# A fused hybrid decoder layer: the order of every engine listed operation by operation, and the places of its rotating buffers listed too

## The chip, the cores and the metric

One core of one Trainium2 chip runs the whole kernel. The metric is the device time in microseconds; the median of three runs of the kernel before is 687.27 us (686.93 to 688.39). The core has five engines that run side by side, each through its own list of instructions: TensorE (PE, matrix products and transposes by a product with the identity), VectorE (DVE), ScalarE (ACT), GpSimd (POOL) and SyncE (SP, which here issues most transfers). An engine takes its instructions strictly in the order of its list and waits on semaphores for what the others produce.

## The reference

One decoder layer for 1024 positions of width 1024, all in float32. A modulation is computed from a conditioning vector, the input is normalised and modulated, and one projection gives the queries, three sets of keys and values, gates, and the input of a state-space mixer. Two mixers follow: attention with three branches (compressed, selected and window keys), 8 heads of 64 in two groups, and a diagonal complex recurrence with 32 groups of 64 states. Both are gated, put side by side, projected, and added to the input.

```python
mod = jax.nn.silu(c) @ w_ada + b_ada
shift, scale, gate = jnp.split(mod, 3, axis=-1)
h = rms_norm(x, norm_g) * (1 + scale[:, None, :]) + shift[:, None, :]
proj = h @ w_in
...
q = rms_norm(q.reshape(B, T, N_HEADS, HEAD_DIM), q_norm_g)
kc = rms_norm(compress(kv_heads(kcr), cmp_pos_k, cmp_w1_k, cmp_w2_k), k_cmp_norm_g)
...
attn = nsa_attention(q, kc, vc, k_slc, kv_heads(vsl), k_win, kv_heads(vwn), gates)
attn = attn * jax.nn.silu(z_a)
y = s5_mixer(u, ssm_a_re, ssm_a_im, ssm_log_dt, ssm_b_re, ssm_b_im, ssm_c_re, ssm_c_im, ssm_d)
y = jax.nn.gelu(y)
y = y * jax.nn.sigmoid(y @ glu_w.astype(jnp.float32) + glu_b.astype(jnp.float32))
ssm = y.astype(x.dtype) * jax.nn.silu(z_s)
mix = jnp.concatenate([attn, ssm], axis=-1) @ w_out
return x + gate[:, None, :] * mix
```

With 16 selected blocks of 64 positions, all 1024 positions are selected, so the selected branch is plain causal attention.

## The kernel before

Most large products are made in three pieces: each float32 operand is split into a rounded part and the rest (names ending in `hi`/`h` and `lo`/`l`), and the products high by high, high by low and low by high are summed in PSUM. So one 128x512 result of eight contraction steps takes 24 matmuls.

The work is cut into 680 jobs, registered by name with the jobs they need (`I("kpan0", ...)`). The names that matter here, in the order of the program:

- Start: `sc0`, `sc1` make silu of the conditioning vector on every partition (`sc`); `ma`, `mb`, `mc` load and use the modulation weights `wada` (a 128x1024 product with `sc`, summed along the row by DVE; `gs` and `sh` are the scale and shift that come of it); `sq0` to `sq7` square rows of x for the norm (some on DVE, some on ACT), `xsc0` and `xsc1` scale x by the norm (L156 on DVE, L258 on ACT), `xb` transposes it on PE (`ptr`, L266) and `h00` to `h71` evacuate it as `hhi`, `hf` (L297) and `hlo`.
- Projections: `kvaw0..7` and `qaw0..7` split weights (`wsp`, L209 on ACT for the high part), `kva`, `kvb`, `qa`, `qb` are the key/value and query products (`ptp`, L331 to L333), `u0` to `u3`, `cmpk`, `cmpv` and `z` use another layout (`pcp`, L352). `kpan0` norms the first keys and rotates them (`ropeb` on DVE, `kr` on POOL, L152); `kpat0` transposes them on PE (`pkt`, L480).
- State-space mixer, for four groups s: `prep`, `tab`, `mats` prepare its matrices (`s5W`, `s5T`, `s5CA`), `scan` runs the recurrence on DVE (`z`), `out` multiplies with it on PE: `py` takes one product with `s5T` (L853) and one with `z` and `s5CA` (L854) for each of eight groups.
- Attention, per row block i and head h: `ha` are the score products (`S`, L1171) and the row maxima on DVE (`st`, L1188), then the exponentials on ACT (`pp`, L1204); `hs` the sums' reciprocals, `hb` and `hc` normalise both branches into `hl` (L1223 on ACT, L149 on DVE) and issue DMA transposes of it (`PT`, from SP); `ub` the products of V with `PT` (`po`, L1264), many small ones by head; `qt` transposes queries, `ca` and `ct` are the compressed branch (`pc`, `mc`, `Sc`, `lc`). Row blocks go 0, 1, 2, 3, 7, 6, 5, 4.
- Output: `wo` splits and gates the output weights (L152 on DVE), `so`, `at` and `ao` are the output products of the two halves (`po`, L1054).

What sets the order: the list `ORD` names the jobs, and their code runs in that order. The tile framework's scheduler then orders each engine's instructions by its own costs, under the data dependencies. Only the start is pinned: `in_order(sp)` holds SP's order from the first load to job `sw`, and `in_order(dve, act)` DVE's and ACT's to job `eo`. Rotating buffers (19 of tag `w4`, 13 of `w2`, 6 of `f2`, two score banks `S` in PSUM, and others) are taken in turn by tag; a tile waits until the tile before it in its place has been read.

Of the kernel before, what the change touches and what calls it, by code (L numbers as in the profile page):

```python
# [21 lines left out]
NT = 8  # L22
# [10 lines left out]
cU3 mats1 xl1 kpat1 kvb7 kpb0 tq kpb1 kpbn0 u2 qaw0 u3 mod0 mod1 prep2 kpbn1 tab1 cVC out0 scan1 out1 tab2 xl2 cmpk
qaw1 cmpv kpbt0 qaw2 mod2 mod3 mod4 mats2 hidk qaw3 qaw4 qaw5 qa0 qa1 qa2 kpbt1 qa3 mod5 qa4 qa5 qaw6 mod6 qaw7 qa6
qa7 qp0 qp1 qpn0 qs0 qpn1 prep3 qs1 tab3 hidv xl3 qw0 scan2 qr0 cz0 mats3 qw1 scan3 qb0 gw qb1 gates mod7 modf cok cov
cmpK z0_0 qb2 scalev qb3 z0_1 qb4 z0_2 out2 qb5 qb6 g2 cz2 qr1 cz1 z0_3 qt01 qt00 qb7 qpb0 qpb1 qpbn0 ca0 qpbn1 z0_4
z0_5 z0_6 z0_7 out3 cz3 kt ha00 ha01 hs01 ha02 hb00 hc00 z1_0 z1_1 ha03 hs03 hb01 hb02 z1_2 z1_3 z1_4 qsb1 qsb0 z1_5
# [12 lines left out]
hb62 ub75 ha64 hc61 hc62 hb63 ha65 ub76 hs65 so4 hb64 hb65 ha66 ha67 ub77 ca5 ub60 ub61 hc63 hc64 so5 qt50 ub62 ha50  # L50
qt51 hs67 hb66 hb67 hc65 qw4 qr4 ub63 so7 hc66 ha51 hc67 hs51 ub64 hb50 hb51 hc50 hc51 so6 ha52 ha53 ha54 ha55 ha56
ub65 hs53 hb52 hb53 ub66 so3 wo00 wo01 wo02 wo03 ct5 hc52 qt41 at3 hc53 ub67 ub50 hs55 hb54 hb55 hc54 ha57 hs57 ca4
ao30 hc55 ao31 ao00 ao01 qt40 hb56 hb57 at1 at2 ao10 ha40 ha41 hs41 hb40 hc56 hb41 hc57 hc40 ha42 ub51 ao11 ha43 ub52
ao20 hs43 hb42 ct4 hb43 hc41 hc42 ao21 ha44 ha45 hc43 ub53 hs45 ub54 at7 ao70 hb44 hb45 ub55 ao71 ha46 ub56 ub57 ub40
at5 at6 ha47 ao50 ao51 ao61 hc44 hs47 ub41 hc45 hb46 hc46 hb47 ao60 ub42 ub43 ub44 ub45 ub46 hc47 ub47 lo
# [11 lines left out]
    wo13="d", xa0="d", xa1="d", xa2="t", xa3="d", xa4="d", xa5="d", xa6="d", xa7="d")  # L67
N4, N2, F2 = 19, 13, 6
# [11 lines left out]

@with_exitstack
def hymba(ctx: ExitStack, tc: tile.TileContext, t, out, dbg=None):
    nc = tc.nc
    pe, act, dve, pool, sp = nc.tensor, nc.scalar, nc.vector, nc.gpsimd, nc.sync
# [36 lines left out]
    def pst(n, name, tag):  # L121
        return psum["pool"].tile([128, n], F32, name=name, tag=tag, bufs=psum[tag])
# [64 lines left out]
    start = ctx.enter_context(ExitStack())  # L187
    start.enter_context(in_order(sp))
# [276 lines left out]
    def kv_norm(kk, i, r1):  # L465
# [7 lines left out]
        rope(kr, k8, lambda k: cs[:, k, i:i + 2, None, :])  # L473
# [417 lines left out]
    def cmp_hidden(b, nm):  # L891
# [14 lines left out]
        pb_ = ws([128, 2], F32, "pb_")  # L906
# [84 lines left out]
    def y_prep(hf, s):  # L991

        if (s, hf) == (0, 0):
            M["y"] = {}
        if hf == 0:
            M["y"][s] = s4([128, 2, 512], F32, "y", 0)
        u_ = f2([128, 512], F32, "pu_")
        y_ = f2([128, 512], F32, "py_")
        dma(y_[:], yd[s][:, 4 * hf:4 * hf + 4, :].rearrange("p i j -> p (i j)"), "e")
        act.activation(u_[:], y_[:], AF.Square, scale=math.sqrt(0.044715))  # L1000
        stt(u_[:], u_[:], 1.0, y_[:], OP.add, OP.mult)
        act.activation(u_[:], u_[:], AF.Tanh, scale=math.sqrt(2.0 / math.pi))
        stt(M["y"][s][:, hf], u_[:], 1.0, y_[:], OP.add, OP.mult)
# [23 lines left out]
    def gate_row():  # L1027
        M["gate"] = gate = cur["f2"].tile([128, 1024], F32, name="gate")
# [337 lines left out]
    first_ = ExitStack()  # L1366
    first_.enter_context(in_order(dve, act))
# [31 lines left out]
    I("eo")(lambda: first_.close())  # L1399
# [114 lines left out]
    def second_pool():  # L1514
        nonlocal pb
# [12 lines left out]
    I("sp", "sw", "u7m", "gates", "qa7", "qb7", "kva7", "kvb7", "u2", "u3", "cmpk", "cmpv", *zall)(second_pool)  # L1528
# [35 lines left out]
    did = set()  # L1564
# [5 lines left out]
    assert did == set(it), set(it) - did  # L1570
# [58 lines left out]
```

## Time and profile before

| what | value |
| --- | --- |
| median of three runs | 687.27 us (686.93 to 688.39) |
| profiled execution, span from its first to its last instruction | 685.9 us |
| mean granted TensorE clock over the span | 0.984 of full speed |
| instructions | 12622 |
| POOL, busy | 152.5 us |
| HBM read, written | 58.10 MB, 18.61 MB |

The trace gives one execution, and no other time of it than the span; around the span lie some 1.4 us of the median. A row of waits reads: engine, what it was about to make and the line, what it waited for, then us in all, times, longest. A row of a timeline reads: start, duration, engine, line, operation, result and operands, and in brackets the idle time before it and what ended it. A matmul's duration overlaps the next one's, so spacing of starts is the measure of its rate.

### The profile page before, as it was taken

The page shows a single profiled execution, that of the slowest core. Times are in us where ns is not written, and L with a number is a line of the kernel's source. Part 1 is how long each engine was busy: PE and PEld are TensorE (multiplying, and loading weights), DVE is VectorE, ACT ScalarE, POOL GpSimd, SP SyncE. Part 2 cuts the span into 40 slices and gives each one's busy share as a digit, 9 for nine tenths or more (in the row PEclk, how much of TensorE's full clock was granted, in tenths as well). Part 3 has the DMA queues.
Part 4 walks back from the last instruction along what each step waited for, and adds up shares of the span by engine and source line. Part 5 has one row for each costly group of instructions (what it writes and reads, how often), then busy time and mean ns, then how long its engine had stood idle before and what let it go on. Part 6 is the DMA issues. An engine that isn't in the chain of part 4 may idle for free.

```text
span 685.9 us, 12622 instructions
## 1 busy us (share of the span) xinstructions
PE 622.1 (91%) x4662; PEld 492.2 (72%) x4662; DVE 570.0 (83%) x1107; ACT 377.1 (55%) x732; POOL 152.5 (22%) x162
## 2 busy tenths in 40 slices
PE   2578998999798999899999999998899999799996
PEld 0356786887687887788788787657687877687785
DVE  6998999688936889986677787998999998898873
ACT  2777432643472152546577586676766855756641
POOL 0163309129232020460111101112001220011010
PEclk9989999999999999999999999999999999999999
DMA  8984222336275642383556969569979599698994
GB/s 319 417 254 101 47 66 55 98 114 172 68 246 169 181 128 70 89 258 93 133 136 111 223 157 205 155 171 221 235 171 215 127 231 225 166 225 197 252 223 86
DMA packets 209759, 116.76 MB, mean 170 GB/s; under 512 B 159073, under 2 KB 188513, under 8 KB 209698
## 3 DMA queue, kind: packets, MB, share of 16 engines
q1 hardware_dynamic: 205858, 109.38, 62.8%
q0 software_dynamic: 3840, 6.57, 4.2%
q8 instruction: 37, 0.61, 0.4%
q14 instruction: 24, 0.20, 0.1%
HBM read 58.10 MB, written 18.61 MB: 112 GB/s over the span
## 4 chain that ended last, share of the span: by engine, by line
PE 45%; DVE 32%; DMA 8%; ACT 6%; issue 6%; POOL 1%; SPq 1%; DVEq 0%; ACTq 0%; POOLq 0%
PE pcp L352 14%; PE po L1054 8%; PE S L1171 7%; DVE hl L149 5%; DMA wada<-in_w_adaT_dram 3%; PE po L1264 3%; DVE st L1188 3%; PE pglu L1016 3%; DVE z L152 2%; DVE wada L149 1%; PE ptp L333 1%; DVE ps L152 1%; PE ptp L332 1%; ACT pp L1204 1%; PE ptp L331 1%
## 5 line engine op out<-in xcount | busy, mean ns | idle before, releaser
L1204 ACT ACTIVATE pp<-S,st 128x640 f32<-128x640 f32 (+7 forms) x128 | 88.6, 700 | 52.1 <-DVE st L1188 40.8
L149 DVE SCALAR_TENSOR_TENSOR hl<-pp,st,hl 128x640 f16<-128x640 f32 (+7 forms) x128 | 101.2, 822 | 6.2 <-ACT hl L1223 6.1
L1223 ACT ACTIVATE hl<-pp,st 128x640 f16<-128x640 f32 (+7 forms) x128 | 85.3, 731 | 8.3 <-DVE st L152 6.3
L1054 PE MATMUL po<-wo,oh 128*128 128x512 f32 x264 | 85.3, 408 | 4.6 <-DVE wo L152 2.9
L352 PE MATMUL pcp<-hhi,wh 128*128 128x512 f32 x208 | 85.1, 409 | 1.3 <-ACT G L887 1.0
L352 PE MATMUL pcp<-hlo,wh 128*128 128x512 f32 x208 | 82.8, 398 | 0.0
L352 PE MATMUL pcp<-hhi,wl 128*128 128x512 f32 x208 | 82.7, 397 | 0.0
L1188 DVE TENSOR_REDUCE st<-S 128x1 f32<-128x1024 f32 (+3 forms) x64 | 57.1, 917 | 3.8 <-PE S L1171 3.7
L1171 PE MATMUL S<-kT,qh 128*128 128x128 f32 (+3 forms) x192 | 59.4, 368 | 0.8 <-ACT pp L1204 0.7
L1054 PEld LDWEIGHTS po<-wo,oh 128*128 128x128 f32 x264 | 48.8, 191 | 15.7 <-DVE wo L152 4.0
L1264 PE MATMUL po<-V,PT 128*128 128x64 f16 x1584 | 59.2, 193 | 0.5 <-DMA PT<-hl 0.5
L331 PE MATMUL ptp<-wsp,hhi 128*128 128x512 f32 x128 | 54.0, 424 | 5.2 <-ACT hhi L297 3.1
L1264 PEld LDWEIGHTS <-PT 128*128 128x128 f16 x1584 | 53.9, 98 | 6.5 <-issue 5.1
L333 PE MATMUL ptp<-wsp,hlo 128*128 128x512 f32 x128 | 54.1, 424 | 3.1 <-POOL hlo L152 3.1
L332 PE MATMUL ptp<-wsp,hhi 128*128 128x512 f32 x128 | 53.8, 420 | 1.9 <-DVE wsp L152 1.0
L1171 PE MATMUL S<-kT,ql 128*128 128x128 f32 (+3 forms) x192 | 53.8, 339 | 0.1
L152 POOL TENSOR_TENSOR qr<-ropeb 128x512 f32<-128x512 f32 x16 | 23.2, 1467 | 125.2 <-DVE ropeb L152 61.6
L1054 PE MATMUL po<-wo,ol 128*128 128x512 f32 x120 | 47.9, 401 | 0.0
L352 PEld LDWEIGHTS pcp<-hhi,wh 128*128 128x128 f32 x208 | 39.6, 190 | 10.1 <-ACT G L887 1.4
L352 PEld LDWEIGHTS pcp<-hlo,wh 128*128 128x128 f32 x208 | 39.2, 189 | 9.2
L352 PEld LDWEIGHTS pcp<-hhi,wl 128*128 128x128 f32 x208 | 39.4, 189 | 8.2
L1171 PEld LDWEIGHTS S<-kT,qh 128*128 128x128 f32 x192 | 33.2, 190 | 14.6 <-issue 9.8
(328 smaller groups left out, 1361.1 us busy)
## 6 DMA issues: line engine op xcount, KB each, us to landing
wada<-in_w_adaT_dram SPq DMA_DIRECT2D x24, 512.0 KB, 7.3
wr<-in_w_in_dram SPq DMA_DIRECT2D x14, 512.0 KB, 4.7
x<-in_x_dram SPq DMA_DIRECT2D x8, 512.0 KB, 6.5
wor<-in_w_out_dram SPq DMA_DIRECT2D x8, 512.0 KB, 5.0
out_dram<-o SPq DMA_DIRECT2D x16, 256.0 KB, 2.5
wraw<-in_w_in_dram SPq DMA_DIRECT2D x15, 256.0 KB, 4.7
xo<-in_x_dram SPq DMA_DIRECT2D x14, 256.0 KB, 3.4
ud<-U SPq DMA_DIRECT2D x4, 512.0 KB, 3.8
```

What stands on the lines that cost most here:

```text
L149: dve.scalar_tensor_tensor(out=o, in0=a, scalar=s, in1=b, op0=o0, op1=o1, **kw)
L152: e.tensor_tensor(out=o, in0=a, in1=b, op=op)
L331: pe.matmul(p, H(k)[:, tsl], w[:, 0, :], start=k == 0, stop=False)
L332: pe.matmul(p, H(k)[:, tsl], w[:, 1, :], start=False, stop=False)
L333: pe.matmul(p, H(k, True)[:, tsl], w[:, 0, :], start=False, stop=k == 7)
L352: pe.matmul(p[:], w[:, k, :], H(k, l)[:, halves(half)], start=(k == 0 and w is hi and not l), stop=(k == 7 and l))
L1054: pe.matmul(p, a[x][:, k, :], w[y][:, halves(n)], start=k == 0 and m == 0, stop=k == 3 and m == 2)
L1171: pe.matmul(R[:, c0:c1], w, x, start=bank not in opened, stop=False, skip_group_check=True)
L1188: dve.tensor_reduce(out=st[br], in_=us[br][0][:, :W], axis=AX.X, op=OP.max, negate=True)
L1204: act.activation(pp[:, :W], R[:, :W], AF.Exp, bias=st[br], accum_out=st4[:, 1, 2 * (h % 2) + br:2 * (h % 2) + br + 1])
L1223: act.activation(hl[:, :W], pp[:, :W], AF.Copy, scale=st[br])
L1264: pe.matmul(o, p, v, start=first, stop=end, skip_group_check=True)
```

## The change

The engines' handles become recorders: a job's code runs first and only notes each operation, by job and engine (`p` PE, `v` DVE, `a` ACT, `g` POOL, `s` SP, `x` the opening of a pool). Tiles are made when an operation that uses them is issued (`Late`). Then a new `ORD` is walked, whose entries name a job, an engine and a count, and each takes the next operations of that job on that engine. The walk stands under `in_order(*engines)`, so each engine's order is the listed one from the first instruction to the last. `SLOTS` lists for every tag which place each tile takes, one character a tile, in the order in which tiles are made. No instruction is added or removed on any engine: 4368 matmuls, 270 transfers issued by SP and 48 by POOL, as before.

```diff
+class Recorder:
+
+    def __init__(self, engine, job, mark):
+        self.real, self.job, self.mark = engine, job, mark
+
+    def __getattr__(self, op):
+        return lambda *a, **k: self.job[-1].setdefault(self.mark, []).append((getattr(self.real, op), a, k))
...
-    pe, act, dve, pool, sp = nc.tensor, nc.scalar, nc.vector, nc.gpsimd, nc.sync
+    pe, act, dve, pool, sp = (Recorder(e, job, m) for e, m in zip(engines, "pavgs"))
...
+    def slot(pool_, tag, shape, dt, name):
+        return Late(lambda: pool_().tile(shape, dt, name=name, tag=f"{tag}{slots[tag].pop(0)}", bufs=1))
...
     def w4(shape, dt, name):
-        return cur["pool"].tile(shape, dt, name=name, tag="w4", bufs=cur["w4"])
+        return slot(lambda: cur["pool"], "w4", shape, dt, name)
...
-    start = ctx.enter_context(ExitStack())
-    start.enter_context(in_order(sp))
...
-        u_ = f2([128, 512], F32, "pu_")
-        y_ = f2([128, 512], F32, "py_")
+        u_ = w2([128, 512], F32, "pu_")
+        y_ = w2([128, 512], F32, "py_")
...
-    for n in ORD:
-        g, deps = it[n]
-        assert n not in did and did.issuperset(deps), ("order", n, [d for d in deps if d not in did])
-        g()
-        did.add(n)
...
+    with in_order(*engines):
+        for part in ORD:
+            n, c = part.split(":")
+            for _ in range(int(c[1:] or 1)):
+                issue(*ops[n][c[0]].pop(0))
```

A line of the list before, and one of the list now, at row block 7 of attention:

```diff
-hb71 hc71 hb72 hc72 ha74 hb73 wo12 wo13 ub34 ub35 ub36 ha75 qt60 hc73 ub37 hs75 hb74 hb75 ub70 ha76 ha77 hs77 ub71 so0
+ha74:v so0:g ha74:p hc72:s ha74:p ub71:p6 at0:a ub71:p6 ub35:p6 ub70:p6 ub71:p6 ub35:p wo10:v ha74:a ub35:p5 qt60:p3
```

Here `ub71` stands ahead of `qt60` and `ha75`, where it stood behind them, and it goes in sixes between other products. This holds for the P·V products (`ub`) all through attention. The matmuls as a whole stand on average 33 places from where they stood, of 4368; DVE's instructions 8.6 of 1080, ACT's 3.8, POOL's 4 and SP's 5. At the start of SP's list, the first split weights and one block of `wada` now stand ahead of x, and two small loads far behind it; ACT's first two squares of the second half of x stand ahead of its scaling of the first half, and its last square behind the first `hhi`. On ACT the splits of `qaw3` and `qaw6` stand ahead of work that was ahead of them.

Three places follow, with the rows of an engine's list before and now. In a row, a name is a tile, a number after it tells tiles of one name apart, and x2 stands for two instructions with the same row; all lines of the changed kernel read L375, the line that issues a recorded operation.

PE at the first key transposes, before: four `pkt` behind the last steps of `kvb6` and four transposes of the first mixer matrices (`pw`).

```order
L796 MATMUL pw<-ident,s5W 128x128 x4
L333 MATMUL ptp<-wsp,hlo_94 128x512
L331 MATMUL ptp<-wsp,hhi_92 128x512
L332 MATMUL ptp<-wsp,hhi_92 128x512
L333 MATMUL ptp<-wsp,hlo_94 128x512
L480 MATMUL pkt<-ident,kr 128x128 x4
L331 MATMUL ptp<-wsp,hhi_92 128x512
L332 MATMUL ptp<-wsp,hhi_92 128x512
L333 MATMUL ptp<-wsp,hlo_94 128x512
L352 MATMUL pcp<-hhi_91,wh_324 128x512
```

And now, behind six products of `u1` (`pcp`) and six of `kvb7`:

```order
L375 MATMUL pcp<-hhi_82,wh_538 128x512
L375 MATMUL pcp<-hhi_82,wl_606 128x512
L375 MATMUL pcp<-hlo_84,wh_538 128x512
L375 MATMUL ptp<-wsp,hhi_82 128x512 x2
L375 MATMUL ptp<-wsp,hlo_84 128x512
L375 MATMUL ptp<-wsp,hhi_82 128x512 x2
L375 MATMUL ptp<-wsp,hlo_84 128x512
L375 MATMUL pkt<-ident,kr 128x128 x4
L375 MATMUL pcp<-hhi_82,wh_538 128x512
L375 MATMUL pcp<-hhi_82,wl_606 128x512
L375 MATMUL pcp<-hlo_84,wh_538 128x512
```

The four `pw` and three `ptp` of `kvb6` now stand behind `pkt`, and more products of the projection `u1` ahead of it. On DVE, preparation of the mixer that stood ahead of the last `ropeb` (five products of `prep0`, nine of `tabf`, the `skip` of `mats0`, a weight split) now stands behind it.

PE at the second group of the mixer's outputs (`out1`), before: the first two `py` stand between `ptp` products of queries, and the first `py` that takes `z` comes 42 matmuls behind the first `py`.

```order
L352 MATMUL pcp<-hhi_92,wh_900 128x512
L352 MATMUL pcp<-hhi_92,wl_901 128x512
L352 MATMUL pcp<-hlo_94,wh_900 128x512
L853 MATMUL py<-s5X,s5T 128x128
L332 MATMUL ptp<-wsp,hhi_91 128x512
L333 MATMUL ptp<-wsp,hlo_93 128x512
L331 MATMUL ptp<-wsp,hhi_91 128x512
L853 MATMUL py<-s5X,s5T 128x128
L332 MATMUL ptp<-wsp,hhi_91 128x512
```

And now, behind compression products (`pcp` of `cmpv`), with the `z` products at once:

```order
L375 MATMUL pcp<-hhi_81,wh_1644 128x512
L375 MATMUL pcp<-hhi_81,wl_1668 128x512
L375 MATMUL pcp<-hlo_83,wh_1644 128x512
L375 MATMUL py<-s5X,s5T 128x128
L375 MATMUL py<-z,s5CA 128x127
L375 MATMUL py<-s5X,s5T 128x128
L375 MATMUL py<-z,s5CA 128x127
```

The first `py` stands 46 matmuls later in PE's list than before (the 645th in place of the 599th), the first that takes `z` five matmuls later.

DVE at the output weights `wo`, in row block 5 of attention, before:

```order
L149 SCALAR_TENSOR_TENSOR hl<-pp,st,hl 128x768
L149 SCALAR_TENSOR_TENSOR hl<-pp,st,hl 128x640
L149 SCALAR_TENSOR_TENSOR za<-za,vsc,pat 128x512
L149 SCALAR_TENSOR_TENSOR hl<-pp,st,hl 128x768
L149 SCALAR_TENSOR_TENSOR hl<-pp,st,hl 128x640
L1188 TENSOR_REDUCE st<-S 128x1 x2
L152 TENSOR_TENSOR wo<-wor,wo 128x1024
L1121 TENSOR_REDUCE mc<-pc_6793 128x8
L152 TENSOR_TENSOR wo<-wor,wo 128x1024
L156 TENSOR_SCALAR mc<-mc 128x8
L152 TENSOR_TENSOR Sc<-pc_6793,mc 128x512
L152 TENSOR_TENSOR wo<-wor,wo 128x1024 x2
```

And now:

```order
L375 SCALAR_TENSOR_TENSOR za<-za,vsc,pat 128x512
L375 SCALAR_TENSOR_TENSOR hl<-pp,st,hl 128x640
L375 TENSOR_REDUCE st<-S 128x1 x2
L375 TENSOR_TENSOR wo<-wor,wo 128x1024 x2
L375 TENSOR_REDUCE mc<-pc_6742 128x8
L375 TENSOR_SCALAR mc<-mc 128x8
L375 SCALAR_TENSOR_TENSOR hl<-pp,st,hl 128x640
L375 TENSOR_TENSOR Sc<-pc_6742,mc 128x512
L375 RECIPROCAL st<-st 128x4
L375 TENSOR_TENSOR wo<-wor,wo 128x1024
L375 TENSOR_TENSOR st<-st,gcol 128x4
L375 TENSOR_TENSOR wo<-wor,wo 128x1024
```

The first two `wo` stand together ahead of the maxima `mc` of the compressed scores, one `hl` of 640 moved behind them, and the last two stand apart with the reciprocal and product of `st` between.

More of the change, by code (lines that the diff above doesn't have):

```diff
@@ L33 @@
[L33 to L37, printed above, removed]
@@ L78, in f32, with __init__, get, __getitem__ @@
     return ap.bitcast(F32)
+class Late:
+    real = None
+    def __init__(self, make):
+        self.make = make
+    def get(self):
+        if self.real is None:
+            self.real = self.make()
+        return self.real
+    def __getitem__(self, at):
+        return Late(lambda: self.get()[at])
+    def __getattr__(self, name):
+        return lambda *a, **k: Late(lambda: getattr(self.get(), name)(*a, **k))
+def now(x):
+    if isinstance(x, Late):
+        return x.get()
+    if isinstance(x, (list, tuple)):
+        return type(x)(now(y) for y in x)
+    return x
+class Recorder:
[3 more added lines that the diff above has]
+        return lambda *a, **k: self.job[-1].setdefault(self.mark, []).append((getattr(self.real, op), a, k))
+def issue(op, a, k):
+    op(*now(a), **{n: now(x) for n, x in k.items()})
 @with_exitstack
@@ L83, in hymba @@
     nc = tc.nc
-    pe, act, dve, pool, sp = nc.tensor, nc.scalar, nc.vector, nc.gpsimd, nc.sync
+    engines = nc.tensor, nc.scalar, nc.vector, nc.gpsimd, nc.sync
+    job = [{}]
+    ops = {"pre": job[-1]}
+    pe, act, dve, pool, sp = (Recorder(e, job, m) for e, m in zip(engines, "pavgs"))
+    later = lambda f: job[-1].setdefault("x", []).append((f, (), {}))
+    slots = {tag: list(text) for tag, text in SLOTS.items()}
+    def slot(pool_, tag, shape, dt, name):
+        return Late(lambda: pool_().tile(shape, dt, name=name, tag=f"{tag}{slots[tag].pop(0)}", bufs=1))
     dbg = dbg or {}
@@ L1492, in hymba, with pool_a, kt @@
     kT = pa = None
-    def kt():
-        nonlocal kT, pa
+    def pool_a():
+        nonlocal pa
         close_pool("s5b")
         pa = open_pool("pa", 1, "right")
-        kT = pa.tile([128, 4, 1024], F32R, name="kT")
+    def kt():
+        nonlocal kT
+        later(pool_a)
+        kT = Late(lambda: pa.tile([128, 4, 1024], F32R, name="kT"))
         for n in range(2):
@@ L1519, in second_pool, with second @@
         pc = open_pool("pc", 1, "left")
-        M["ps"] = pc.tile([128, NT, 1024], F32, name="ps")
-    pb = None
+    def second():
+        later(second_pool)
+        M["ps"] = Late(lambda: pc.tile([128, NT, 1024], F32, name="ps"))
+    pb = pc = None
     order = OA + OB
@@ L1563, in hymba, with record @@
         I(f"ct{i}", f"ca{i}")(lambda i=i: cmp_trans(i))
-    did = set()
-    for n in ORD:
-        g, deps = it[n]
-        assert n not in did and did.issuperset(deps), ("order", n, [d for d in deps if d not in did])
-        g()
-        did.add(n)
-    assert did == set(it), set(it) - did
+    def record(n):
+        if n not in ops:
+            g, deps = it[n]
+            for d in deps:
+                record(d)
+            job.append({})
+            g()
+            ops[n] = job[-1]
+    for n in it:
+        record(n)
+    with in_order(*engines):
[3 more added lines that the diff above has]
+                issue(*ops[n][c[0]].pop(0))
+    assert not any(q for o in ops.values() for q in o.values())
     for p in ("ps1", "pc", "pf", "pb", "hp", "work", "pa", "s5a"):
```

343 lines of the change are left out of this document (301 added, 42 removed).

## The prediction

> **What bounds the kernel now.** I read the page first: the busy time of each engine, then the shares of the chain that ended last.
>
> ```profile
> span 685.9 us, 12622 instructions
> PE 622.1 (91%) x4662; PEld 492.2 (72%) x4662; DVE 570.0 (83%) x1107; ACT 377.1 (55%) x732; POOL 152.5 (22%) x162
> PE 45%; DVE 32%; DMA 8%; ACT 6%; issue 6%; POOL 1%; SPq 1%; DVEq 0%; ACTq 0%; POOLq 0%
> ```
>
> TensorE (PE) is busy for 91% of the span and holds 45% of the chain; VectorE (DVE) holds 32%. No instruction is taken away by the change, so it can only win idle time. I therefore went to PE's waits (us in total, times, longest) and then to windows of the span.
>
> ```profile
> PE ptr L266 <- DVE x L156: 15.4, 1, 15.4
> PE S L1171 <- ACT pp L1204: 8.5, 13, 1.9
> PE po L1054 <- DVE wo L152: 2.9, 2, 2.1
> PE pkt L480 <- POOL kr L152: 2.9, 1, 2.9
> PE py L854 <- DVE z L152: 2.4, 1, 2.4
> PE ptp L331 <- ACT wsp L209: 2.1, 2, 1.7
> PE po L1264 <- DMA PT<-hl: 0.5, 2, 0.2
> ```
>
> These rows, the ones that the change touches, add up to 34.7 us of the 64 (685.9 − 622.1) in which PE is idle; the largest is the start, before any product. The windows give, after start and length, each engine's busy time in the order PE, weight load, DVE, ACT, POOL, then PE's granted clock, the DMA share and GB/s.
>
> ```profile
> 20.00:40.00 20.00, 11.87 (x40) 7.88 (x40) 18.57 (x44) 13.63 (x22) 5.88 (x4) 1.00 1.05 399
> 80.00:100.00 20.00, 20.00 (x95) 15.97 (x94) 20.00 (x88) 6.35 (x9) 2.29 (x5) 1.00 0.29 84
> 100.00:120.00 20.00, 17.11 (x90) 13.71 (x89) 19.90 (x30) 6.30 (x11) 15.82 (x14) 0.91 0.18 47
> 180.00:200.00 20.00, 17.05 (x92) 14.34 (x91) 11.86 (x21) 8.98 (x23) 5.14 (x12) 0.91 0.51 152
> 600.00:620.00 20.00, 19.48 (x186) 15.94 (x187) 19.94 (x32) 11.91 (x20) 2.83 (x2) 0.92 0.90 212
> ```
>
> Three kinds of stretch: from 20 to 40 us the DMA engines are full; around 100 and 600 us DVE has no idle time to give; around 180 us every engine has some. A new order wins most in the last kind, and in the others only where the work in front of a late result is shortened.
>
> One more thing hangs on PE's gaps. I cut windows at four of the places where the clock fell below 1.00:
>
> ```profile
> 108.24:111.65 3.41, 3.41 (x12) 2.72 (x12) 3.41 (x6) 0.89 (x2) 3.29 (x4) 0.50 0.02 5
> 186.75:190.16 3.41, 3.41 (x18) 3.41 (x18) 3.00 (x7) 0.59 (x1) 0.83 (x2) 0.50 0.48 135
> 217.47:220.88 3.41, 3.41 (x10) 2.62 (x9) 1.75 (x3) 2.41 (x5) 0.00 (x0) 0.50 0.80 320
> 599.76:603.17 3.41, 3.08 (x7) 2.49 (x8) 3.38 (x6) 2.29 (x4) 0.00 (x0) 0.50 1.48 274
> ```
>
> Each is 3.41 us at half clock, right behind a gap of PE: half of 3.41, 1.7 us of PE's time, is lost where PE is the late engine. The Trainium skill (TensorE: Matmul & The Clock Gate, Part 1: The HAM clock gate) says that the clock falls after at least one idle window of about 3.4 us and warns of gaps longer than that. The gaps here are 2.9, 2.4, 1.7 and 2.1 us, all shorter, so the trace does not bear that threshold out; by the rule such gaps would cost no clock, and the sum below would be 3.4 us smaller.
>
> **The change part by part.** Matmuls, vector operations and transfers stay the same in number and shape; each engine's order and each buffer's place change. Durations are of the one profiled execution, whose span of 685.9 us is 1.4 below the median of the runs shown (687.27). Negative terms are time won.
>
> *Start.* The rows are two DVE scalings of x, the fourth square of ACT, the first h and the first weight product.
>
> ```profile
> 20.73 1.41 DVE L156 TENSOR_SCALAR x<-x,rstd 128x1024 f32<-128x1024 f32 x2
> 23.18 1.05 ACT L243 ACTIVATE sq<-x 128x1024 f32<-128x1024 f32 x1
> 24.22 0.77 ACT L297 ACTIVATE hhi<-ptr,sh,gs 128x512 fp32r<-128x512 f32 x1
> 25.04 0.80 PE L331 MATMUL ptp<-wsp,hhi 128*128 128x512 f32 x1 [1.52 <-ACT hhi L297]
> 28.04 1.42 DVE L156 TENSOR_SCALAR x<-x,rstd 128x1024 f32<-128x1024 f32 x2
> ```
>
> On ACT the last square now stands behind the first h, and two stand ahead of the scaling of x; on DVE the scaling comes about 1.0 us earlier (my sum of the work ahead). So h is ready about 2.7 us sooner, by the squares moved behind it and the earlier scaling. But the second scaling (28.04) has two more column sums (1.23 us each) ahead of it and comes no earlier, x lands behind two more weight transfers, and the queues are full here. Between 0 and −2.7, I take half: **−1.4**.
>
> *First key transposes (pkt).* PE waits 2.9 us for the rotated keys, which POOL adds:
>
> ```profile
> 103.70 3.91 POOL L152 TENSOR_TENSOR kr<-ropeb 128x512 f32<-128x512 f32 x2 [19.67 <-DVE ropeb L152]
> 105.13 2.77 DVE L152 TENSOR_TENSOR kk<-kk,gains 128x256 f32<-128x256 f32 x2
> 107.67 0.66 PE L480 MATMUL pkt<-ident,kr 128*128 128x128 f32 x4 [2.89 <-POOL kr L152]
> ```
>
> The order takes about 5.1 us of DVE work (table and matrix preparation) from ahead of ropeb, and puts about 1.1 us more PE work ahead of pkt. 5.1 + 1.1 covers 2.9 even if half of what DVE saves is lost to waiting for inputs. With the half-clock stretch behind it: −2.9 − 1.7 = **−4.6** (between 0, if DVE's inputs set the time, and −4.6).
>
> *Second scan's outputs (out1).*
>
> ```profile
> 170.37 0.40 PE L352 MATMUL pcp<-hhi,wl 128*128 128x512 f32 x1
> 170.61 0.40 PE L352 MATMUL pcp<-hlo,wh 128*128 128x512 f32 x1
> 171.86 0.49 PE L853 MATMUL py<-s5X,s5T 128*128 128x128 f32 x2 [0.86 <-ACT zw L827]
> 185.79 0.49 PE L854 MATMUL py<-z,s5CA 128*128 128x127 f32 x2 [2.36 <-DVE z L152]
> ```
>
> A product is issued every 0.24 us (170.61 − 170.37) at full clock. The first two py products stand 46 products later than before, behind compression products, so they lose their 0.9 us wait. The product that waits for z has about 1.5 us more PE work ahead of it, and DVE's scan ends after 1.5 us less work: 3.0 against a wait of 2.4, just covered. −0.9 − 2.4 − 1.7 (clock) = **−4.9**; if the scan is not earlier, 0.9 + 1.5 = −2.4.
>
> *Query weights.*
>
> ```profile
> 215.29 0.73 PE L331 MATMUL ptp<-wsp,hhi 128*128 128x512 f32 x2 [1.65 <-ACT wsp L209]
> 216.75 0.50 PE L332 MATMUL ptp<-wsp,hhi 128*128 128x512 f32 x1 [0.73 <-DVE wsp L152]
> ```
>
> ACT's splits for these now stand ahead of 9 and 7 us of its other work, so both waits go: **−2.4**. The half-clock stretch behind them (217.47) I leave in, since the DMA share there is 0.80 at 320 GB/s; between 0, if the transfer is late, and −4.1.
>
> *Output weights (wo).*
>
> ```profile
> 597.10 1.21 DVE L152 TENSOR_TENSOR wo<-wor,wo 128x1024 fp32r<-128x1024 f32 x1
> 598.36 0.50 PE L1054 MATMUL po<-wo,oh 128*128 128x512 f32 x1 [2.13 <-DVE wo L152]
> 600.09 0.80 PE L1054 MATMUL po<-wo,oh 128*128 128x512 f32 x1 [0.78 <-DVE wo L152]
> ```
>
> DVE reaches the first two wo about 3.5 and 4.1 us of work sooner, the last two 1.4; PE reaches the product 1.1 us sooner. Of 2.9 us waited about 2.0 goes: **−2.0** (0 to −4.6 with the clock). DVE is full here, so what is moved behind is late next.
>
> *Scores.* 8.5 us in 13 waits for ACT's exponentials, which leave a score bank free. P·V products, before in one run a head, now stand in sixes between and inside score products. DVE's maxima and PE's scores both come 1 to 2 us earlier by work, so most waits stay: **−1.5** (from −8.5, all filled, to +8.5, as many again).
>
> *Buffers and waits.* Buffer places are listed rather than taken by turn; that adds no instruction, and its cost I put at nothing, hidden under PE's 91%. If a place listed is freed late, it is the slower rival's kind of wait.
>
> **Sum:** −1.4 − 4.6 − 4.9 − 2.4 − 2.0 − 1.5 = −16.8. PE at the next point meets other producers that were only just early, and DVE's full stretches hold back what is won ahead of them; I take off a quarter: −12.6. 685.9 − 12.6 = 673.3, and 1.4 to the median: **675 us**.
>
> **The rivals.**
>
> *Waits merely move.* DVE at 20.00 of 20 us (80 to 100) and 19.94 (600 to 620) speaks for it: PE's gaps won earlier reappear at the next DVE result. Against it: at 180 to 200 us DVE has 8 us idle. It gives 685 to 689, 687 taken.
>
> *Larger gain.* If the sixes of P·V products also fill the score waits and the smaller gaps: the terms in full, −16.8, the rest of the score waits, −7.0, the clock terms left out (1.7 each at 217 and 600), −3.4: 685.9 − 27.2 + 1.4 = 660.
>
> *Slower: P·V ahead of its transposes.* P·V products read probabilities that a DMA transpose turned round.
>
> ```profile
> 468.48 3.37 DMA PT<-hl
> L1237 SPq DMA_TRANSPOSE PT<-hl x3: 1650/2751/3012, 475.2 to 482.0; - x3
> DMA to landing us min/median/max: 4.7/5.1/5.3
> ```
>
> They wait 0.5 us in all today. In the row shown landing takes about 5 us from issue. The change issues the first P·V products of a head ahead of score products (ub71 ahead of qt60 and ha75, where it was behind). The mechanism decides where PE reaches such a six sooner than about 5 us after its transposes' issue: PE's queue stands, the scores behind that six are late, then DVE's maxima. At half of 5.1, 2.5 us, in 8 of the 64 heads: +20 on −12.6: 685.9 + 7.4 + 1.4 = 695.
>
> *DVE beside POOL.* The two kk products above took 2.77 us while POOL ran, against 0.45 for one of the same form:
>
> ```profile
> 101.33 0.45 DVE L152 TENSOR_TENSOR kk<-kk,gains 128x256 f32<-128x256 f32 x1
> ```
>
> So this meeting cost 2.77 − 2 × 0.45 = 1.9 us of DVE. Six more meetings in full stretches would take 11 of the 12.6 back: 686. The Trainium skill (SBUF — State Buffer, Who interferes with whom) has it that a DVE instruction with two SBUF inputs and a GpSimd instruction that reads SBUF exclude each other, whichever starts first; the rows agree. The order moves POOL by only a few places, so I give it little.
>
> *The order is not what it says.* Excluded by the rows of the order above.
>
> **How the numbers follow.** My forecast (668 to 683) 0.55, the larger gain 0.17 (a third of it below 660), waits that move 0.10, P·V too early 0.13, DVE beside POOL 0.05. The predicted time is the forecast's, 675. From 660 to 691 about 0.16 is left out. A measurement of this kernel can tell about 0.2%, 1.4 us, from no change. Faster: 0.55 + 0.17 + 0.03 from the waits that move = 0.75. Same: 0.05 of the same rival + 0.03 of the POOL case = 0.08. Slower: 0.13 + 0.02 + 0.02 = 0.17.
>
> **What would show it.** Right: PE's wait at pkt, the z wait of out1 and the wo waits are gone from the table of waits, with the clock at 1.00 near 108, 186 and 600 us; PE's busy sum falls a little (no half clock) and the span by more. Wrong: the same us under other names (DVE st, DVE z) in the 500 to 620 windows, or "PT<-hl" among the largest waits. If the start's 15.4 us falls by more than 1.4 with it, the start was mis-sized.

## The result and the profile after

The changed kernel takes 666.86 us (median of 4 runs, 664.34 to 668.17), the kernel before 687.10 (4 runs, 685.47 to 688.39). The ratio is 0.970, with a 95% interval of 0.9666 to 0.9734: 20 us faster, where 12 were forecast; the time lies 1.1 us below the forecast's range of 668 to 683. The profiled execution took 667.23 us, its span 665.5; of the spans, 685.9 − 665.5 = 20.4 us are to be found.

The page after, the same lines as before:

```profile
span 665.5 us, 12576 instructions
PE 616.1 (93%) x4662; PEld 490.8 (74%) x4662; DVE 560.7 (84%) x1107; ACT 379.6 (57%) x732; POOL 141.0 (21%) x162
PE 12%; DVE 5%; DMA 3%; ACT 2%; issue 1%; SPq 0%; ACTq 0%; DVEq 0%
```

PE's idle time falls from 64 to 49 us, and its busy sum by 6: together they are the 20.4 us. The chain of this page is followed back over 23% of the span only, so it isn't compared. The waits of PE after (us in total, times, longest):

```profile
PE ptr L375 <- DVE x L375: 16.1, 4, 10.8
PE pcb L375 <- DVE ones L375: 5.8, 1, 5.8
PE ptr L375 <- ACT hf L375: 5.6, 4, 2.2
PE po L375 <- DMA PT<-hl: 3.7, 4, 2.7
PE pk L375 <- DVE s5CA L375: 2.1, 1, 2.1
PE S L375 <- ACT pp L375: 1.8, 3, 0.9
PE py L375 <- DVE z L375: 0.6, 1, 0.6
PE po L375 <- DVE wo L375: 0.6, 1, 0.6
```

The wait for `kr` ahead of `pkt` is gone, z fell from 2.4 to 0.6, `wo` from 2.9 to 0.6, the score banks from 8.5 to 1.8. Four waits are new or longer: `ones` at the start (`pcb` is the product that spreads the conditioning vector with this constant), `hf` ahead of the transposes of x (2.1 us in one wait before), `s5CA`, and `PT`, which rose from 0.5 to 3.7. "PT<-hl" among the largest waits was one of the signs by which the prediction would have shown itself wrong, and it shows at one place, below. The windows of before, and one at 460 us (PE, weight load, DVE, ACT, POOL, clock, DMA share, GB/s):

```profile
20.00:40.00 20.00, 9.05 (x24) 5.00 (x24) 18.94 (x47) 13.20 (x20) 3.77 (x3) 1.00 0.99 357
80.00:100.00 20.00, 17.92 (x85) 14.26 (x84) 19.70 (x78) 4.66 (x8) 4.07 (x7) 1.00 0.18 41
100.00:120.00 20.00, 20.00 (x100) 15.91 (x98) 14.21 (x30) 6.28 (x9) 11.56 (x12) 0.92 0.25 71
180.00:200.00 20.00, 19.40 (x133) 16.77 (x133) 15.28 (x26) 7.77 (x18) 9.19 (x23) 1.00 0.54 166
460.00:480.00 20.00, 16.51 (x259) 13.49 (x258) 16.80 (x19) 14.33 (x23) 2.94 (x2) 0.91 1.07 231
600.00:620.00 20.00, 20.00 (x202) 16.32 (x202) 17.26 (x27) 14.23 (x28) 3.35 (x2) 1.00 0.95 184
```

At 180 us PE now has 19.4 of 20 us, where it had 17.1; at 100 and 600 us DVE, full before, has 6 and 3 us free, while from 80 to 100 us it is still full (19.70). At 20 us PE does less than before. The half-clock stretches:

```profile
55.45:58.86 3.41, 3.41 (x11) 2.66 (x10) 3.07 (x19) 1.67 (x4) 1.03 (x1) 0.50 0.70 158
99.82:103.23 3.41, 3.41 (x12) 2.55 (x11) 3.41 (x11) 1.28 (x2) 0.00 (x0) 0.50 0.00 0
468.46:471.87 3.41, 3.41 (x43) 3.22 (x40) 3.41 (x4) 3.41 (x7) 1.53 (x1) 0.50 1.09 225
```

But for the last microseconds of either run these are three of 3.41 us, 10.2 in all, against five places with 20.5 us before (6.83 at 40 us and the four shown): PE gets back about half of the difference, 5 us. This share belongs to the two executions that were profiled: in two of the four executions of the changed kernel the mean clock was 0.996 and 0.997, which leaves room for little half clock but that at the end.

To find the rest I counted PE's instructions in each run's own order, each at its spacing in the kernel before, and compared when the same amount of product work was done. The jobs move past each other, so this is a better ruler than the end of one job; with another choice of the spacings a stage comes out up to about 1 us otherwise.

| stage (time in the kernel before, us) | forecast | measured |
| --- | --- | --- |
| start, to 83 | −1.4 | +2.6 |
| first keys, 83 to 135 | −4.6 | −0.9 |
| 135 to 165 | 0 | +0.9 |
| second scan's outputs and query weights, 165 to 239 | −7.3 | −11.1 |
| projections and first attention blocks, 239 to 468 | part of −1.5 | −4.7 |
| 468 to 487 (`ub71`) | 0 | +2.9 |
| attention, 487 to 590 | part of −1.5 | −4.5 |
| output weights, 590 to 613 | −2.0 | −4.1 |
| to the end | 0 | −1.5 |
| given back | +4.2 | in the rows above |
| sum | −12.6 | −20.4 |

### The profile page after: what moved, and what is told of

Read it like the earlier page. It is cut to its first block, busy times and chain, and to the rows that moved or that the text cites. A ratio compares the mean times of both kernels' runs of the same rounds, so it can differ in the third digit from the quotient of the medians.

```text
span 665.5 us, 12576 instructions
## 1 busy us (share of the span) xinstructions
PE 616.1 (93%) x4662; PEld 490.8 (74%) x4662; DVE 560.7 (84%) x1107; ACT 379.6 (57%) x732; POOL 141.0 (21%) x162
## 5 line engine op out<-in xcount | busy, mean ns | idle before, releaser
L375 ACT ACTIVATE pp<-S,st 128x640 f32<-128x640 f32 (+7 forms) x128 | 88.8, 697 | 46.0 <-DVE st L375 37.5
L375 DVE SCALAR_TENSOR_TENSOR hl<-pp,st,hl 128x640 f16<-128x640 f32 (+7 forms) x128 | 97.8, 781 | 13.0 <-ACT hl L375 12.8
L375 ACT ACTIVATE hl<-pp,st 128x640 f16<-128x640 f32 (+7 forms) x128 | 89.4, 730 | 30.4 <-DVE st L375 17.3
L375 DVE TENSOR_REDUCE st<-S 128x1 f32<-128x640 f32 (+7 forms) x96 | 83.5, 884 | 15.8 <-PE S L375 15.7
L375 PE MATMUL ptp<-wsp,hhi 128*128 128x512 f32 x256 | 86.0, 418 | 0.9 <-ACT hhi L375 0.9
L375 PE MATMUL po<-wo,oh 128*128 128x512 f32 x264 | 84.5, 405 | 2.5 <-ACT wo L375 0.8
L375 PE MATMUL pcp<-hhi,wh 128*128 128x512 f32 x208 | 85.4, 410 | 0.0
L375 PE MATMUL pcp<-hhi,wl 128*128 128x512 f32 x208 | 82.1, 395 | 0.4 <-DVE wl L375 0.4
L375 PE MATMUL pcp<-hlo,wh 128*128 128x512 f32 x208 | 82.4, 396 | 0.0
L375 PE MATMUL po<-V,PT 128*128 128x64 f16 x1584 | 62.6, 194 | 3.7 <-DMA PT<-hl 3.7
L375 PEld LDWEIGHTS <-PT 128*128 128x128 f16 x1584 | 56.1, 99 | 11.7 <-issue 6.5
L375 PE MATMUL S<-kT,qh 128*128 128x128 f32 (+3 forms) x192 | 60.3, 372 | 0.2 <-ACT pp L375 0.2
L375 PEld LDWEIGHTS po<-wo,oh 128*128 128x128 f32 x264 | 48.3, 190 | 13.0 <-ACT oh L375 1.1
L375 PEld LDWEIGHTS ptp<-wsp,hhi 128*128 128x128 f32 x256 | 48.4, 197 | 11.8 <-ACT hhi L375 1.3
L375 PE MATMUL S<-kT,ql 128*128 128x128 f32 (+3 forms) x192 | 53.8, 337 | 0.0
L375 PE MATMUL ptp<-wsp,hlo 128*128 128x512 f32 x128 | 52.3, 409 | 0.8 <-POOL hlo L375 0.8
L375 PE MATMUL po<-wo,ol 128*128 128x512 f32 x120 | 47.4, 396 | 0.0
L375 PEld LDWEIGHTS pcp<-hhi,wh 128*128 128x128 f32 x208 | 39.3, 189 | 9.0 <-ACT U L375 0.8
L375 PEld LDWEIGHTS pcp<-hlo,wh 128*128 128x128 f32 x208 | 39.1, 188 | 9.1
L375 PEld LDWEIGHTS pcp<-hhi,wl 128*128 128x128 f32 x208 | 39.2, 188 | 8.5 <-DVE wl L375 0.8
L375 POOL TENSOR_TENSOR qr<-ropeb 128x512 f32<-128x512 f32 x16 | 21.3, 1348 | 111.7 <-DVE ropeb L375 40.6
L375 PEld LDWEIGHTS S<-kT,ql 128*128 128x128 f32 x192 | 36.3, 189 | 3.5
```

What stands on the lines that cost most here:

```text
L375: op(*now(a), **{n: now(x) for n, x in k.items()})
```

## The experiments

Each kernel was timed beside the kernel before on its own chip (medians there 686.6 to 688.9), so I compare ratios; 0.01 is 6.9 us. The changed kernel's own is 0.970.

**Order or places.** Two kernels issue a listed order with places found by a rule: at a tile's first use, the place whose last use lies longest back.

```diff
-        return Late(lambda: pool_().tile(shape, dt, name=name, tag=f"{tag}{slots[tag].pop(0)}", bufs=1))
+        x = Late(lambda: pool_().tile(shape, dt, name=name, tag=f"{tag}{x.place}", bufs=1), None, tag)
...
+                    free = [(h.get(p, -1), p) for p in range(COUNT[x.tag]) if h.get(p, -1) < k]
+                    x.place = min(free)[1]
+                    h[x.place] = last[x]
```

The first has the order that the scheduler gave the kernel before, its list opening so:

```diff
-kvaw0:s pre:s mb0:s pre:s lb:s pre:s2 kvaw0:a pre:s2 kvaw0:g mb2:s lb:s pre:v ma0:s sc0:p ma7:s xl_1:s sc0:a s5l:s
+pre:g0 pre:s0 pre:v0 s5p:v98-99 cmpK:g0 pre:s1-3 sc1:p0 pre:s4 ll:v1 pre:s5 cmpk:s0 cmpv:s0 sc0:p0 sc1:a0 hidk:s0
```

> The order of before, operation by operation on every engine, issued through the recorders of the changed kernel; places of rotating buffers by a rule (the place whose last use lies longest back), not the list. Theory, that the order of the engines makes the gain: about 687 us, as before (684 to 690). Rival, that recording, fewer waits or the listed places bring a part of it: 668 to 680.

694.48 us, ratio 1.0057 (1.0023 to 1.0091): listing an order and issuing it through recorders wins nothing by itself. The second keeps the new order:

> The new order as it is, places by the same rule instead of the list. Theory (order): 667 us or a little less, 663 to 667, since the constant 'ones' then gets a place of its own at the start. Rival (the listed places matter): 672 or more.

673.12 us, ratio 0.977 (0.9735 to 0.9804). With the same rule the order alone makes 1.0057 − 0.977 = 0.0287, 20 us: nearly the whole gain, as the theory has it. But both times miss the theory's ranges, by 4.5 and 6.1 us, the second inside the rival's range: places matter too, since my rule costs about 0.6% against the turn of before and 0.7% against the list. The new order with places taken by turn was not run, so what the listed places are worth against the turn stays open. In the trace of the second, the place shows at the query weights: loads (SPq), ACT's split, DVE's, PE.

```profile
212.71 0.37 SPq L418 DMA_DIRECT2D wraw<-in_w_in_dram  x1
213.03 0.62 ACT L418 CAST wsp<-wraw 128x512 fp32r<-128x512 f32 x1 [1.94 <-DMA wraw<-in_w_in_dram]
213.68 1.29 DVE L418 TENSOR_TENSOR wsp<-wraw,wsp 128x512 fp32r<-128x512 f32 x2 [4.88 <-ACT wsp L418]
215.03 0.51 PE L418 MATMUL ptp<-wsp,hhi 128*128 128x512 f32 x1 [2.94 <-DVE wsp L418]
```

and in the changed kernel:

```profile
208.57 0.38 SPq L375 DMA_DIRECT2D wraw<-in_w_in_dram  x1
208.81 0.62 ACT L375 CAST wsp<-wraw 128x512 fp32r<-128x512 f32 x1 [1.92 <-DMA wraw<-in_w_in_dram]
209.46 1.29 DVE L375 TENSOR_TENSOR wsp<-wraw,wsp 128x512 fp32r<-128x512 f32 x2 [1.73 <-ACT wsp L375]
```

The same load is issued 4.1 us later, the order being the same, where PE's products at 200 us stand only 1 us later. It is late because SP's list is: an entry ahead of it, a load of `w1s` (the first weights of the compression's two layers, in the same rotating buffer `w2`), is issued at 204.26 in place of 199.49, and the profile puts 4.0 us of SP's wait there down to the transfer `yd<-Y`. So a load that has to wait holds the transfers behind it in SP's list. `Y` is a tile of `w2` too; that it lay in the place that `w1s` takes is what I infer, as the trace doesn't name places.

**Which part of the order.** Three kernels take the operations of one stretch in the order of before among themselves, with places by the rule, and so stand against 0.977.

> The operations that the new order has up to 168 us stand in the order of before among themselves, the rest in the new order; places by the rule, so it is compared with the new order with such places (673.1 us where before was 688.9). Theory (the new start is worth nothing, since PE's products there come 2.6 us later than before): 669 to 673 us. Rival (the new start prepares what follows): 678 or more.

672.28 us, 0.9768 (0.9696 to 0.9839): no gain of the start is seen, as the theory had it, though by the interval 4.9 us either way could hide.

> Only the operations that the new order has between 168 and 232 us (compression, second scan's outputs, query weights) stand in the order of before among themselves; places by the rule, compared with 673.1 us. Theory (about 5 us of the gain with these places, 10 with the listed ones, lie here): 677 to 684 us. Rival (a gap removed here only comes back later): 671 to 675.

675.62 us, 0.9811 (0.9749 to 0.9873): 2.8 us, between the two and inside the noise; with places by the rule this stretch has a gap in either order, so the kernel tells little.

> The new order up to 460 us, the order of before among the operations behind it; places by the rule, compared with 673.1 us. Theory (8 us of the gain lie behind 460 us): 679 to 683 us. Rival (DVE is full there and sets the time in any order): 672 to 675.

686.11 us, 0.9965 (0.9933 to 0.9996): 13 us, more than the theory's 6 to 10; what the joint of the two orders costs by itself was not tested. Its trace has the waits of before again (5.0 us in 11 for the score banks, 3.2 us for `wo`), with 6.83 us of half clock at 478 and at 597 us.

**The second scan's outputs.** Ten compression products go from ahead of `out1` to behind it, on PE alone.

```diff
-scan1:v cmpv:p3 scan1:v cmpv:a cmpv:p2 cmpv:a cmpv:p scan1:v cmpv:a cmpv:p2 scan1:v cmpv:p out1:p tab2:v out1:p2
+cmpv:a2 scan1:v cmpv:a scan1:v out1:p tab2:v out1:p2 scan1:v out1:p3 tab2:v mod2:s out1:p2 qaw1:v out1:p2 out1:a
```

> The changed kernel with ten compression products moved on PE from ahead of the second scan's outputs to behind them. Theory (PE's work ahead of z removes the wait, not an earlier scan): PE waits about 2.9 us for z near 184 us, with a half-clock stretch, 668.5 to 671.5 us. Rival (what stands behind is late anyway and takes the loss up): 666 to 668.

672.11 us, 0.9769 (0.9738 to 0.98), 0.6 above the theory's range. The z product in its trace, and the window behind it:

```profile
186.98 0.80 PE L375 MATMUL py<-z,s5CA 128*128 128x127 f32 x2 [2.94 <-DVE z L375]
186.29:193.12 6.83, 6.14 (x29) 6.14 (x30) 5.10 (x9) 0.59 (x1) 1.76 (x4) 0.50 0.28 89
```

A wait of 2.9 us is followed by 6.83 us of half clock: 2.9 + 3.4 = 6.3, and by the count of products this kernel stays 6 us behind the changed one to the end. The execution profiled is the slowest of its five; by the ratios the kernel is 4.7 us behind. The theory holds, in this execution with a second half-clock stretch that it had not counted, and what is lost here does not come back.

**The output weights.** On DVE the first two `wo` move 2.4 us of work back:

```diff
-at1:s wo01:a ca4:p wo00:v ca4:p hc52:s ca4:p2 wo02:a ca4:p ub51:p4 wo01:v ub51:p8 ub67:p6 hc53:s ub51:p3 hb53:a ub51:p3 ao30:p3 ca4:v
+at1:s wo01:a ca4:p2 hc52:s ca4:p2 wo02:a ca4:p ca4:v2 ub51:p12 ub67:p6 hc53:s ub51:p3 hb53:a hc53:v ca4:v wo00:v wo01:v ub51:p3 ao30:p4
```

> The changed kernel with one change on DVE: the first two wo stand behind mc, mc, hl of 640 and Sc, as before, 2.4 us of work later. Theory (a late wo costs PE its wait and a half-clock stretch): PE waits 2 to 3 us for wo near 580 us, 669 to 671 us. Rival (DVE is full, so what moves ahead gives it back): 666 to 668.

671.33 us, 0.9764 (0.9735 to 0.9793), just over the theory's range. In its trace:

```profile
582.77 0.79 PE L375 MATMUL po<-wo,oh 128*128 128x512 f32 x1 [4.66 <-DVE wo L375]
582.19:585.60 3.41, 2.83 (x7) 2.20 (x8) 3.41 (x6) 1.43 (x3) 0.00 (x0) 0.50 0.51 115
```

The wait is 4.66 us, longer than the theory's 2 to 3. DVE was full there before, and yet the order of its work decides: 4.4 us by the ratio, where the two intervals just miss each other.

**The scores.** 50 of the 96 entries of row maxima move behind the next instruction of DVE's list; one of them:

```diff
-ub12:p2 ub14:p2 ha23:v ub14:p3 z4_6:p4 hc16:v z4_6:p2 hc15:v
+ub12:p2 ub14:p5 z4_6:p4 hc16:v ha23:v z4_6:p2 hc15:v
```

> The changed kernel with 50 of the 96 entries of row maxima moved behind the next instruction of DVE's list. Theory (the score waits went because the maxima, and so the exponentials, come sooner): PE's waits for pp rise from 1.8 us to 5 or more, 670 to 678 us. Rival (there is slack between maxima and score banks): under 669.

675.06 us, 0.9825 (0.9791 to 0.9858). Its wait for the banks:

```profile
PE S L373 <- ACT pp L373: 6.6, 9, 1.5
```

8.6 us by the ratio for a shift of one place each. 4.8 us of it are score waits (6.6 against 1.8), and its trace has as many half-clock stretches as the changed kernel's, so the other 3.8 us are not traced. The maxima's places on DVE are what took most of the score waits away. Next, P·V: every head's products stand at the place of their last group. Their new order changes some of the P·V sums, so the attention output is not the reference's; the work is the same.

```diff
-ha74:v so0:g ha74:p hc72:s ha74:p ub71:p6 at0:a ub71:p6 ub35:p6 ub70:p6 ub71:p6 ub35:p wo10:v ha74:a ub35:p5 qt60:p3
+ub70:p18 wo10:v ha74:a ub35:p24 qt60:p3 wo12:s qt60:p so0:p wo13:s qt60:a ha74:v at0:g so0:p3 ha74:a ub71:p24 ha75:p3
```

> The changed kernel with listed places; in PE's list each head's P.V products (but for the one that opens a sum) stand together at the place of their last group, so 280 groups become about 120. Theory (groups in sixes fill the waits for score banks): PE's waits for ACT's pp rise from 1.8 us by 4 to 7, 671 to 676 us. Rival (the score waits went because DVE and ACT come earlier): under 669.

669.61 us, 0.9724 (0.9664 to 0.9784), between the two. But the wait decides:

```profile
PE S L358 <- ACT pp L358: 2.1, 4, 0.8
```

2.1 us against 1.8: the sixes are not what filled the score waits, so the theory falls. (In PE's list 280 groups became 148, not about 120.)

**The rival that came true in one place.** In the changed kernel PE reaches `ub71` before its transposes have landed:

```profile
468.28 1.18 PE L375 MATMUL po<-V,PT 128*128 128x64 f16 x21 [2.68 <-DMA PT<-hl]
```

The next kernel moves its first 24 products behind `ha75`:

```diff
-ha74:v so0:g ha74:p hc72:s ha74:p ub71:p6 at0:a ub71:p6 ub35:p6 ub70:p6 ub71:p6 ub35:p wo10:v ha74:a ub35:p5 qt60:p3
+ha74:v so0:g ha74:p hc72:s ha74:p at0:a ub35:p6 ub70:p6 ub35:p wo10:v ha74:a ub35:p5 qt60:p3
```

> The changed kernel with the first 24 P.V products of ub71 moved behind qt60, so0 and ha75 in PE's list. Theory (the wait for PT at 468 us is lost time): the wait of 2.7 us and the half clock behind it go, 662.5 to 665 us. Rival: PE meets the next late producer (ACT's oh or the score banks) at once, and the time stays at 666 to 667.

666.32 us, 0.9687 (0.9636 to 0.9739): no gain. Its trace has a new wait a little later:

```profile
472.43 0.51 PE L375 MATMUL po<-wo,oh 128*128 128x512 f32 x1 [2.07 <-DVE wo L375]
```

In this execution DVE's next result is late too, and 6.83 us of half clock follow from 473.89. The time is the rival's; its reason is less sure, since the execution profiled took 673.06 us at a mean clock of 0.983 and the other three 665.99 to 666.64 at 0.992 to 0.996.

**The start.** In the list of places, the first weights and `ones` share place 0 of `w2`, so DVE's first instruction waits until POOL has read the weights.

```diff
-        "001234325676489A9BC951CA6A16B78C50166C1B781259A66C102A9B4A987C153460C957A3129CA536871B403A87615C3C0A"
+        "0C1234325676489A9BC951CA6A16B78C50166C1B781259A66C102A9B4A987C153460C957A3129CA536871B403A87615C3C0A"
```

> The changed kernel with one character of the w2 list changed: 'ones' takes place C, not place 0 behind the first weights. Theory: the first sc on DVE comes at about 5 us instead of 8.6, and PE's products up to 165 us come 1 to 3 us sooner: 664 to 666 us. Rival: the transfers set the start, so the first product stays near 24.6 us and the time at 667.

667.29 us, 0.9673 (0.963 to 0.9716). `sc` comes 2.4 us sooner (6.24 for 8.59), not at about 5, the first weight product 0.5 us (24.16 for 24.62), and at 15 us of product work both stand at 51 us: what DVE wins there is lost by then, as the rival has it, with the transfers full (a DMA share of 0.99 from 20 to 40 us in the changed kernel).

**A version that may be faster than both.** With the place of `ones` as above, the first six products of `pk` go behind 15 others on PE:

```diff
-kpan0:v u7m:p prep0:v mats0:p3 u0:a kpan0:v mats0:p2 tabf:v mats0:p tabf:v
+kpan0:v u7m:p prep0:v u0:a kpan0:v tabf:v2
...
-kvb4:p2 tabf:v kvb4:p tabf:v
+kvb4:p2 tabf:v kvb4:p mats0:p6 tabf:v
```

> The changed kernel with 'ones' in place C and the first six products of the first mixer matrices (pk) moved behind 15 key and projection products on PE. Theory (the wait of 2.1 us for s5CA near 99 us and the half clock behind it are lost time): both go, 662.5 to 665 us. Rival (kpan0 and DVE set the pace there, as PE waits at the next key transposes): 666 to 668.

664.59 us, 0.9661 (0.9632 to 0.969), the fastest seen; its interval overlaps the changed kernel's, so the 2.7 us between the ratios are not shown by the times. The trace, at the same window of the changed kernel and then of this one, and this one's next wait:

```profile
95.00:105.00 10.00, 7.92 (x36) 5.94 (x34) 9.85 (x24) 2.98 (x3) 0.00 (x0) 0.83 0.31 99
```

```profile
95.00:105.00 10.00, 10.00 (x66) 8.13 (x65) 9.98 (x26) 4.04 (x5) 0.46 (x1) 1.00 0.41 125
111.47 0.66 PE L375 MATMUL pkt<-ident,kr 128*128 128x128 f32 x4 [1.70 <-POOL kr L375]
```

The wait and the half clock are gone in this execution; 1.7 us come back at `pkt`, as the rival had it, without half clock. By the count of products, 3 us remain to the end.

## Why the prediction was right, and where its sizes were off

The direction and its mechanism held: the order alone makes 20 us, and it does so by taking PE's waits and the half-clock stretches behind them. The size did not: the sum of −12.6 was 7.8 us short, above all in the scores and in the quarter taken off, and three terms, the start, the first keys and the scores, had a step wrong. Term by term:

- **Start (−1.4), wrong in sign.** PE is 2.6 us behind at 83 us. Seen from the order, work moved from ahead of the first weight product; in the trace that product came at 24.62 instead of 25.04, but PE had 9.05 us of work in the window from 20 us instead of 11.87. I valued DVE's and ACT's lists; `ones_apart` shows that an earlier DVE gains nothing there, and `old_first` that the start of before gains nothing either. Part of the loss may go with the places: at 83 us the traces with listed places stand 1.7 to 3.3 us behind the kernel before, and the three with the same start and places by the rule 0.5 to 1.5. Which transfer or place sets the start stays open.
- **First keys (−4.6), −0.9.** Their own wait went as said. The step that failed is that nothing took its place: ahead of it, `pk` waits 2.1 us for `s5CA`, with 1.7 us of clock, 3.8 together; −4.6 + 3.8 = −0.8. The new order has DVE's preparation behind the keys, and I had not asked what waits for the preparation. `best` shows it: with `pk` moved back, this wait and its half clock are gone.
- **Second scan and query weights (−7.3), −11.1.** The waits went, but not quite as I had it: I covered the z wait half by more of PE's work ahead of it and half by an earlier scan, and the scan did not end sooner (its last z starts at 186.5 in the trace after, 185.8 before). PE's own order does it, as `out1_back` shows, where ten products moved back bring the wait from 0.6 to 2.94. What the sum lacked is the half-clock stretch at 217 us, which I left in and which went too (1.7), and three smaller waits of this stage that no term had and that are gone (for `G` 1.0, a load of `wsp` 0.8, `kh` 0.6): −7.3 + 0.6 − 1.7 − 2.4 = −10.8.
- **Output weights (−2.0), −4.1.** The term was put without the clock, though the half-clock stretch stood among the rows; 2.3 (2.9 − 0.6) + 1.7 is about what was measured.
- **Scores (−1.5), −9.2** for the two stretches that hold attention (the first also holds projections), before the 2.9 lost at `ub71`. The step that failed: I counted DVE's work ahead of a maximum and found 1 to 2 us for both sides, so that the waits would stay. They fell by 6.7 us; `maxima_later` shows that a shift by one place of 50 maxima is enough to bring 4.8 of them back.
- **A quarter given back (+4.2), seen at two named places only.** They are `s5CA` (2.1 us of wait) and `PT` (2.7), each with a half-clock stretch, and stand in the rows of their stages. Elsewhere nothing came back: in `out1_back` and `wo_back` a loss stays to the end, so I take it that a gain does too. DVE's stretches at 100 and 600 us were full in that order, not in any.
- **Buffer places (0), not settled.** I put their cost at nothing. Against the rule the list is worth 0.7%, about 5 us, and one shared place (`ones`) costs a wait of 5.8 us at the start that the time doesn't show; against the turn of before the new order was not run.
- **Rivals.** P·V ahead of its transposes came true at the place named, once: 2.7 us and a half-clock stretch, not eight times. DVE beside POOL seems to have come true once, with a larger price (below), under cover of the gain. The larger gain, 660, came closest: its mechanism, the score waits, was right, its cause, the sixes, was not.

On the gate of the clock, the Trainium skill (TensorE: Matmul & The Clock Gate, Part 1: The HAM clock gate) gives about 3.4 us of idle as the bound. In these runs single waits of 2.08 (`pk`), 2.68, 2.94 and 4.66 us were followed by half clock, and one of 1.70 us (`best`, at `pkt`) was not; the measurement decides. But the length of a wait alone doesn't decide it: one of 3.47 us, in the new order with places by the rule, was followed by none. Its row, and three windows:

```profile
474.26 0.79 PE L418 MATMUL po<-V,PT 128*128 128x64 f16 x21 [3.47 <-DMA PT<-hl]
469.09:472.50 3.41, 1.71 (x34) 1.34 (x30) 3.41 (x4) 2.55 (x3) 0.78 (x1) 1.00 1.33 145
472.50:475.91 3.41, 1.65 (x41) 1.65 (x42) 3.41 (x4) 1.67 (x3) 0.89 (x1) 1.00 1.27 203
475.91:479.32 3.41, 3.23 (x27) 2.21 (x25) 1.58 (x3) 3.41 (x7) 1.63 (x1) 1.00 1.07 233
```

In each trace all changes of the clock lie on one grid with steps of 3.41 us; in the trace after, 55.45, 99.82 and 468.46 are 13 and 108 steps apart. The grid cuts this wait in two, and PE is idle for 1.70 us of one step and 1.76 of the next. I cut the fourteen traces into the steps of their grids, from 30 us on. All 39 full-clock steps in which PE was idle for 1.94 us or more were followed by half clock; of those with less, seven were, with 1.52 to 1.87 us, and others of up to 1.90 us were not. So what counts here is PE's idle time within a step, with the border between 1.5 and 1.9 us, and where the grid lies against a wait is luck that differs between executions.

## What to carry to other kernels

A gap of 2 to 3 us on TensorE cost up to twice its length here where the clock halved behind it, which hangs on how the gap lies in the clock's steps; list those gaps first and price them with and without the clock. When a listed order moves work away from ahead of a late result, ask who waits for the work that moved. An engine that is busy all the time in a trace may still have its results in a bad order: a shift by one place of 50 row maxima cost 8.6 us.

## What was not expected of the hardware

A DVE product that takes 0.55 us at its shortest in the same trace took 6.49 in the changed kernel, beside POOL's products:

```profile
162.00 6.49 DVE L375 TENSOR_TENSOR s5tab<-ta,tb 128x384 f32<-128x384 f32 x1
162.25 3.79 POOL L375 TENSOR_TENSOR kr<-ropeb 128x512 f32<-128x512 f32 x3
165.99 1.06 POOL L375 TENSOR_TENSOR ta<-s5P,s5c 128x512 f32<-128x512 f32 x1
167.01 1.05 POOL L375 TENSOR_TENSOR tb<-s5P,s5c 128x512 f32<-128x512 f32 x1
168.52 0.56 DVE L375 TENSOR_TENSOR ta<-s5f,s5x 128x384 f32<-128x384 f32 x1
```

It ended when the fifth POOL product in a row had (167.01 + 1.05 = 168.06, and the next DVE row starts at 168.52). The Trainium skill (SBUF — State Buffer, Who interferes with whom) says that the later of two such instructions waits until the first has finished; here it waited for five, and by the rows DVE's had even started first (starts on POOL are rough). The 5.9 us lost are more than the lead of 1.5 us that I had forecast for the second scan and that did not come. I made no kernel that keeps the two apart, so the cause rests on the rows.

Executions of one kernel also differ by their clock: the changed kernel's four spans were 662.6 to 666.1 us at mean clocks of 0.987 to 0.997. A difference of 3 us between two single executions says little here.
